# Gate and up projections as Strassen quads over both token halves, and a down projection that stays in PSUM

## The chip, the cores and the metric

The kernel runs on one core of one Trainium2 chip. The time is the device time of one execution in microseconds (us), and the number that counts is the median of several runs. All that is said of single instructions comes from one profiled execution of the kernel before. The engines are PE (TensorE, the matmuls), DVE (VectorE), ACT (ScalarE), POOL (GpSimd) and SP (SyncE, which issues the DMAs).

## The reference

Two transformer layers and a second block run over 1024 tokens of width 1024. Each layer has a mixer and a gated feed-forward part (FFN); the second block has an mLSTM branch and an S5 branch, whose recurrence needs tables made from its parameters.

```python
def swiglu(h, w_gate, w_up, w_down):
    return (jax.nn.silu(h @ w_gate) * (h @ w_up)) @ w_down      # 1024 -> 2816 -> 1024

for layer in range(2):
    h = rmsnorm(x, mix_pre_g[layer])
    m = even_mixer(h, ...) if layer == 0 else odd_mixer(h, ...)  # odd: (gelu(gate) * rg_lru(conv(xr))) @ w_out
    x = x + rmsnorm(m, mix_post_g[layer])
    h = rmsnorm(x, ffn_pre_g[layer])
    x = x + rmsnorm(swiglu(h, ...), ffn_post_g[layer])
# second block: h = x + rmsnorm((g1 * mlstm(...) + g2 * s5(...)) @ w_o)
# s5: a = exp(lam * dt), s_t = a * s_(t-1) + q B u_t, y = Re(C s) + D u
```

## The kernel before, in words

Features lie on the partitions, and the tokens are two halves of 512. Every fp32 operand is held as a high and a low part, so that the product of a 128x128 block of weights with a 128x512 block of activations is three matmuls (L151, L152, L153: high by high, high by low, low by high). A "unit" is 128 output features of one half: 24 matmuls for a depth of 1024.

Weights come by one DMA for each unit into a tile `raw` (two buffers), are rounded to the high part by ACT (L137), and DVE makes the low part (L139) into `wsp` (four buffers). Activations are split in the same way by `split` (L161 on ACT, then L165 on DVE or L163 on POOL or DVE).

`ffn` (L355) takes one half at a time. It makes the gate unit `pg` and the up unit `pu` of 4 or 6 hidden tiles, splits the hidden tiles (L161, L165), and then multiplies this group by its part of the down weights: 8 output units `pd`, each added to an fp32 tile `macc` in SBUF by DVE (L385). Four to six such groups make one half. The rmsnorm of the other half's next input runs beside the last group.

Work beside the matmuls comes from Python generators. `start(g, rate)` puts one in a list, each `tick` emits `rate` further steps of it, and `drain(g)` emits all that is left at once. The order of emission is the order of priority by which a scheduler fills the queue of each engine; a queue is then worked off in order. `early(n)` gives instructions an earlier priority (the loads and splits of weights).

The tables of the S5 branch come from the generator `s5_tables` (L952). It has a head of small DVE instructions, then a loop on DVE, ACT and PE over 16 groups (transposes and products `s5pt`, `s5pk` on PE, tiles `s5zr`, `s5zf`, `s5W`, `s5E`), and at last tables of rotations `s5R` on POOL alone (L1104 to L1117), two groups at a time. Before, it is started here:

```python
        self.layer0(lambda h, *m: self.finish(h, *m, "mix_post_g", 0), side)
        bg = self.start(self.s5_tables(), 1.5)
        self.ahead = 90
        self.drain(first[0])
        self.drain(ffn(0, 1, ("mix_pre_g", 1), (2, 4, 4, 4, 4, 4)))
        self.drain(bg)
```

The mixer of layer 1 follows. Of each head it makes two conv input units `pxr`, two gate units `pg` and the recurrence. `gelu2` (L448) is ACT, POOL (a `tensor_scalar`, L453), DVE, ACT, DVE in a row on a tile `gl`; the PSUM bank of `pg` is free only after its last step.

Of the kernel before, what the change touches and what calls it, by code (L numbers as in the profile page):

```python
# [21 lines left out]
NT = 8  # L22
T = 512
# [13 lines left out]

class Model:
    def __init__(self, ctx, tc, io, slots=24, nraw=2, nwsp=4, nt2=12):
# [3 lines left out]
        self.nslots, self.nraw, self.nwsp, self.nt2 = slots, nraw, nwsp, nt2  # L43
# [17 lines left out]
    def tick(self, n=1):  # L61
        """Emit the next steps of every background generator, each at its own rate."""
# [41 lines left out]
    def t2(self, name, shape=(128, T), dt=F32, tag="t2", bufs=None):  # L104
        return self._t(shape, dt, tag, bufs or self.nt2, name)
# [19 lines left out]
    def wtile(self, src, first=False):  # L125
        """src: [128, nk, n] in DRAM. Returns a tile [128, (hi, lo), 8, 128]."""
        nc = self.nc
        nk = src.shape[1]
        with self.early(self.ahead):
            raw = self.p.tile([128, 8, 128], F32, tag="raw", bufs=self.nraw, name="raw")[:, :nk]  # L130
            nc.sync.dma_start(raw, src)
        with self.early(self.ahead):
            sp = self.p.tile([128, 2, 8, 128], F32R, tag="wsp", bufs=self.nwsp, name="wsp")
            if first:
                nc.gpsimd.tensor_scalar(sp[:, 0, :nk], raw, 1.0, 0.0, ALU.mult, ALU.add)
            else:
                nc.scalar.activation(sp[:, 0, :nk], raw, AF.Copy)  # L137
        with self.early(self.ahead):
            nc.vector.tensor_tensor(sp[:, 1, :nk], raw, f(sp[:, 0, :nk]), ALU.subtract)  # L139
        return sp  # L140

# [3 lines left out]
    def mm3(self, ps, sp, xs, wk0=0, order=None, part=(0, None), bg=0):  # L145
        """ps (+)= the three products of every pair of tiles; part: which of them, in their order."""
        nc = self.nc
        order = order or range(len(xs))
        for i, k in list(enumerate(order))[slice(*part)]:
            h, l = sp[:, 0, wk0 + k], sp[:, 1, wk0 + k]  # L150
# [6 lines left out]
    def split(self, src, name, scale=1.0, dst=None, low=None):  # L157
        """hi/lo pair of src*scale (src fp32 in SBUF or PSUM)."""
# [10 lines left out]
    def sumsq_step(self, acc, src):  # L169
        nc = self.nc  # L170
        q = self.t2("sq", tag="sq", bufs=2)
# [1558 lines left out]
```

## Time and profile before

| | before |
|---|---|
| median of 3 timed runs | 3301.34 us (3300.61 to 3302.1) |
| span of the profiled execution, first to last instruction | 3297.8 us |
| PE busy | 3226.6 us, 98% |
| DVE busy | 2109.4 us, 64% |
| ACT busy | 1383.9 us, 42% |
| POOL busy | 380.3 us, 12% |
| mean granted clock of PE | 0.995 |

The span is that of one execution, without what lies ahead of its first and behind its last instruction; the median is 3.5 us longer, and this difference is taken as what lies around the span. A busy share is a mean over stages that have different limits, so the stage that a change touches is read by itself.

### The profile page before, as it was taken

Reading aid. Unit: us, or ns where it says so; the run is one execution under the profiler, and the core shown is the slowest. Engines: PE = TensorE matmul, PEld = TensorE weight load, DVE = VectorE, ACT = ScalarE, POOL = GpSimd, SP = SyncE. Lnnn points to the kernel's source line nnn. Section 1 sums busy time; section 2 is a strip of 40 time slices with the busy share of each in tenths; the row PEclk is TensorE's granted clock in tenths of the full one; section 3 lists DMA queues with packets and bytes.
Section 4 is the critical chain, followed back from the end, with each engine's and each line's share of the span. In section 5 each row is a group of like instructions: output and inputs, shape, how many; then the busy total and the mean of one; then the engine's idle time right before and its main releaser. Section 6 shows DMA issues by size and latency. Waiting matters only on the chain.

```text
span 3297.8 us, 41400 instructions
## 1 busy us (share of the span) xinstructions
PE 3226.6 (98%) x14848; PEld 2636.9 (80%) x14848; DVE 2109.4 (64%) x3911; ACT 1383.9 (42%) x2228; POOL 380.3 (12%) x720
## 2 busy tenths in 40 slices
PE   8999999999999999999999999999999999999998
PEld 5777788888788887878888888887888888788786
DVE  8668748667965479596544553348688888633633
ACT  4646544334522247575322332224455444323322
POOL 4011100000393002011000000000111110100000
PEclk9999999999999999999999999999999999999999
DMA  5444324434534344334433343237545444334533
GB/s 179 131 138 136 103 90 142 128 114 140 191 111 139 104 124 144 102 122 134 147 96 97 121 141 97 89 107 251 184 128 177 135 153 149 123 97 158 160 93 102
DMA packets 186429, 435.20 MB, mean 132 GB/s; under 512 B 23400, under 2 KB 48168, under 8 KB 186224
## 3 DMA queue, kind: packets, MB, share of 16 engines
q1 hardware_dynamic: 186224, 432.56, 41.8%
q8 instruction: 117, 1.92, 0.2%
q14 instruction: 88, 0.72, 0.1%
HBM read 364.19 MB, written 64.06 MB: 130 GB/s over the span
## 4 chain that ended last, share of the span: by engine, by line
PE 79%; DVE 11%; issue 4%; ACT 3%; DMA 2%; POOL 1%; SPq 0%; DVEq 0%; ACTq 0%; POOLq 0%
PE pg L153 6%; PE pg L152 6%; PE pg L151 6%; PE pu L151 5%; PE pu L153 5%; PE pu L152 5%; PE pd L152 4%; PE pd L153 4%; PE pd L151 4%; PE po L152 3%; PE po L151 3%; PE po L153 3%; DVE wsp L139 2%; PE pya L152 1%; PE pya L153 1%
## 5 line engine op out<-in xcount | busy, mean ns | idle before, releaser
L137 ACT ACTIVATE wsp<-raw 128x1024 fp32r<-128x1024 f32 (+3 forms) x614 | 566.1, 923 | 1161.6 <-issue 332.2
L139 DVE TENSOR_TENSOR wsp<-raw,wsp 128x1024 fp32r<-128x1024 f32 (+3 forms) x618 | 680.6, 1103 | 544.0 <-ACT wsp L137 539.7
L151 PE MATMUL pg<-xs,wsp 128*128 128x512 f32 x1088 | 425.3, 391 | 4.8 <-DVE xc L443 2.7
L152 PE MATMUL pg<-xs,wsp 128*128 128x512 f32 x1088 | 424.9, 391 | 1.1 <-POOL xs L163 1.1
L153 PE MATMUL pg<-xs,wsp 128*128 128x512 f32 x1088 | 424.6, 390 | 0.9 <-DVE wsp L139 0.9
L151 PE MATMUL pu<-xs,wsp 128*128 128x512 f32 x760 | 297.4, 391 | 0.0
L152 PE MATMUL pu<-xs,wsp 128*128 128x512 f32 x760 | 296.4, 390 | 0.0
L153 PE MATMUL pu<-xs,wsp 128*128 128x512 f32 x760 | 296.3, 390 | 0.0
L151 PE MATMUL pd<-hid,wsp 128*128 128x512 f32 x704 | 275.8, 392 | 0.5 <-DVE th L370 0.4
L152 PE MATMUL pd<-hid,wsp 128*128 128x512 f32 x704 | 275.3, 391 | 0.8 <-DVE hid L165 0.6
L153 PE MATMUL pd<-hid,wsp 128*128 128x512 f32 x704 | 274.3, 390 | 0.0
L151 PEld LDWEIGHTS pg<-xs,wsp 128*128 128x128 f32 x1088 | 204.3, 188 | 48.5 <-issue 3.4
L152 PEld LDWEIGHTS pg<-xs,wsp 128*128 128x128 f32 x1088 | 204.3, 188 | 45.1 <-POOL xs L163 2.7
L153 PEld LDWEIGHTS pg<-xs,wsp 128*128 128x128 f32 x1088 | 204.3, 188 | 43.3 <-DVE wsp L139 1.6
L163 POOL TENSOR_TENSOR xs<-xt,xs 128x512 fp32r<-128x512 f32 x36 | 54.2, 1504 | 1408.8 <-ACT xs L161 1393.0
L370 DVE TENSOR_TENSOR th<-th,pu 128x512 f32<-128x512 f32 x88 | 60.4, 687 | 179.0 <-PE pu L153 178.6
L153 PEld LDWEIGHTS pu<-xs,wsp 128*128 128x128 f32 x760 | 142.6, 188 | 29.7
L152 PEld LDWEIGHTS pu<-xs,wsp 128*128 128x128 f32 x760 | 142.7, 188 | 28.8
L151 PEld LDWEIGHTS pu<-xs,wsp 128*128 128x128 f32 x760 | 142.8, 188 | 28.7
L152 PEld LDWEIGHTS pd<-hid,wsp 128*128 128x128 f32 x704 | 132.2, 188 | 31.9 <-DVE hid L165 5.3
L151 PEld LDWEIGHTS pd<-hid,wsp 128*128 128x128 f32 x704 | 132.1, 188 | 28.3 <-ACT hid L161 0.8
L153 PEld LDWEIGHTS pd<-hid,wsp 128*128 128x128 f32 x704 | 132.2, 188 | 27.1
(637 smaller groups left out, 6620.0 us busy)
## 6 DMA issues: line engine op xcount, KB each, us to landing
raw<-in_w_in_dram SPq DMA_DIRECT2D x96, 512.0 KB
raw<-in_wg_dram SPq DMA_DIRECT2D x88, 512.0 KB
raw<-in_wu_dram SPq DMA_DIRECT2D x88, 512.0 KB
xt<-xres SPq DMA_DIRECT2D x120, 256.0 KB
raw<-in_wd_dram SPq DMA_DIRECT2D x96, 256.0 KB
raw<-in_wd_dram SPq DMA_DIRECT2D x48, 384.0 KB
raw<-in_ev_in_dram SPq DMA_DIRECT2D x32, 512.0 KB
xres<-xt SPq DMA_DIRECT2D x64, 256.0 KB
```

The source lines that it names most:

```text
L137: nc.scalar.activation(sp[:, 0, :nk], raw, AF.Copy)
L139: nc.vector.tensor_tensor(sp[:, 1, :nk], raw, f(sp[:, 0, :nk]), ALU.subtract)
L151: nc.tensor.matmul(ps, h, xs[k][:, 0], start=i == 0, stop=False)
L152: nc.tensor.matmul(ps, h, xs[k][:, 1], start=False, stop=False)
L153: nc.tensor.matmul(ps, l, xs[k][:, 0], start=False, stop=i == len(xs) - 1)
L163: (low or nc.vector).tensor_tensor(t[:, 1], src, f(t[:, 0]), ALU.subtract)
L370: nc.vector.tensor_tensor(th, th, pu, ALU.mult)
```

## The change

**Gate and up.** The units are now made in quads: two units by both token halves by both halves of the depth, by a form of Strassen's product with 7 instead of 8 products of half the depth (12 matmuls each). Operands are sums of weight blocks (`wquad`: four 128x512 sums on POOL for each quad) and sums of activations (`sum_steps`: DVE and POOL, with new splits). A quad makes 84 matmuls where there were 96. Both halves of x must be there for this, so six of the eleven pairs of hidden tiles (`ffn_first`) are begun with half 0 alone while half 1 is finished; one product of these is kept in DRAM (`m1d`), and the rest of such a quad is 5 products. There are 22 quads in each of the two layers.

**Down.** Hidden tiles go to DRAM (`hidd`), are loaded again (`hid_steps`, tile `hl`), and are split there. `ffn_down` adds all 22 of them in one PSUM bank, so the additions to `macc` go.

**Buffers.** `t4` has 27 slots instead of 24, `t2` 18 instead of 12, and takes in the tiles that had tags of their own (`xt`, `sq`, `hf`, `p`, `P`); `raw` has 3, `wsp` 8 of half the size, and weights are split in halves of 128x512.

**S5 tables.** The loop takes 2 groups of parameters at a time instead of 4, and the rotations 1 group instead of 2: twice as many instructions of half the size. The generator is started beside `ffn_down` alone, and what is left is emitted at once behind it.

```diff
+    def prod(self, ps, w, xs, start, bg):
...
+        for k in range(n):
+            h, l = w.h(k), w.l(k)
+
+            nc.tensor.matmul(ps, h, xs[k][:, 0], start=start and k == 0, stop=False, skip_group_check=not start)
+            nc.tensor.matmul(ps, h, xs[k][:, 1], start=False, stop=False, skip_group_check=not start)
+            nc.tensor.matmul(ps, l, xs[k][:, 0], start=False, stop=k == n - 1, skip_group_check=not start)
...
+    def quad(self, w, B, sink, bank, m1=None, bg=0.3):
+
+        nc = self.nc
+        Y, Z, X = bank("qy"), bank("qz"), bank("qx")
+        rest = m1 is not None
+        cp = lambda o, i: nc.scalar.activation(o, i, AF.Copy)
+        if not rest:
+            self.prod(Y, w["a11"], B["b11"], True, bg)
+            m1 = self.t2("qm1")
+            cp(m1, Y)
+        self.prod(Z, w["s1"], B["t1"], True, bg)
+        v5 = self.t2("qv5")
+        cp(v5, Z)
+        self.prod(Y, w["s2"], B["t2"], rest, bg)
...
+        self.prod(Z, w["s4"], B["b22"], False, bg)
+        sink(0, 1, Z, u2)
+        self.prod(Y, w["s3"], B["t3"], False, bg)
...
+        nc.gpsimd.tensor_tensor(v5, v5, u3, ALU.add)
+        sink(1, 1, v5, None)
...
+            self.prod(X, w["a12"], B["b21"], True, bg)
+            sink(0, 0, X, m1)
+            self.prod(Y, w["a22"], B["t4"], False, bg)
+            sink(1, 0, Y, None)
...
+    def hid_steps(self, h, out):
+        for j in range(FFT):
+            t = self.t2("hl")
+            self.nc.sync.dma_start(t, self.hidd[h][j])
+            out.append(self.split(t, "hid", 0.5))
+            yield
...
+    def ffn_down(self, l, h, hid, n0=0):
...
+                for k in range(n):
+                    h_, l_, x = sp.h(k), sp.l(k), hid[k0 + k]
+                    nc.tensor.matmul(ps, h_, x[:, 0], start=k0 + k == 0, stop=False)
+                    nc.tensor.matmul(ps, h_, x[:, 1], start=False, stop=False)
+                    nc.tensor.matmul(ps, l_, x[:, 0], start=False, stop=k0 + k == FFT - 1)
+                    self.tick(1 / 8)
+            nc.scalar.activation(mt, ps, AF.Copy)
+            ss = self.sumsq_step(ss, mt)
...
+    def ffn(self, l, B, keep, pre, hook, F, done=0, beside=()):
...
+        for j in range(done, F):
+            if j == done + 3:
+                self.finished()
+                nb = self.start(self.ffn_sums(*pre, B, keep), 1.0)
+            self.ffn_first(l, 2 * j, B, None)
+        self.drain(nb)
...
+        for j in range(F, n):
+            self.ffn_quad(l, 2 * j, B, False)
+        for j in range(F):
+            if j == F - 1:
+                nb = self.start(self.hid_steps(0, hid[0]), 3.0)
+            self.ffn_quad(l, 2 * j, B, True)
+        self.drain(nb)
+        self.ahead = 90
+        bg = self.start(beside, 2.0) if beside else None
+        m, ss = self.ffn_down(l, 0, hid[0])
+        hid[0].clear()
+        nb = self.start(self.hid_steps(1, hid[1]), 3.0)
+        self.drain(nb)
+        self.finish(0, m, ss, "ffn_post_g", l)
+        nb = self.start(chain(self.after(self.fin), hook()), 1.0)
+        m, ss = self.ffn_down(l, 1, hid[1])
+        self.drain(nb)
+        if bg:
+            self.drain(bg)
+        self.finish(1, m, ss, "ffn_post_g", l)
...
+        GT = 2
...
-        for g0 in range(0, 16, 2):
-            R = self.t4("s5R", [128, 2, 2, 256], F32)  # (gt, cos/sin, b)
+        for g0 in range(16):
+            R = self.t2("s5R", [128, 1, 2, 256])
...
-        bg = self.start(self.s5_tables(), 1.5)
-        self.ahead = 90
-        self.drain(first[0])
-        self.drain(ffn(0, 1, ("mix_pre_g", 1), (2, 4, 4, 4, 4, 4)))
-        self.drain(bg)
-        # layer 1 mixer
+        self.ffn(0, B[0], keep[0], ("ffn_pre_g", 0), hook("mix_pre_g", 1), 6, 1, self.s5_tables())
```

How the change moves instructions is seen in the queues at the border between layer 0's FFN and layer 1's mixer. On POOL of the kernel before, the last rotations stand ahead of four splits of the normed x (`xs`, two of them left out here), and then come the mixer's first two gelu steps (`gl`):

```order
L1115 TENSOR_TENSOR s5rt_10164<-s5R_10161,s5c_4840 128x256
L1116 TENSOR_TENSOR s5rt_10164<-s5R_10161,s5c_4840 128x256
L1117 TENSOR_TENSOR s5R_10161<-s5rt_10164 128x2x128
L163 TENSOR_TENSOR xs_10973<-xt_10970,xs_10973 128x512
...
L163 TENSOR_TENSOR xs_11131<-xt_11128,xs_11131 128x512
L453 TENSOR_SCALAR gl_11302<-gl_11302 128x512
L453 TENSOR_SCALAR gl_11345<-gl_11345 128x512
L163 TENSOR_TENSOR yo_11429<-gl_11302,yo_11429 128x512
```

On POOL of the changed kernel, the same two steps (now L710) stand among and behind the rotations of all 16 groups; first the place of `gl_12488`, then that of `gl_12531`, the last rotation ahead of it:

```order
L1371 TENSOR_TENSOR s5R_12238<-s5rt_12241 128x4
L1369 TENSOR_TENSOR s5rt_12294<-s5R_12291,s5c_8430 128x4
L1370 TENSOR_TENSOR s5rt_12294<-s5R_12291,s5c_8430 128x4
L710 TENSOR_SCALAR gl_12488<-gl_12488 128x512
L1371 TENSOR_TENSOR s5R_12079<-s5rt_12082 128x64
L1371 TENSOR_TENSOR s5R_12132<-s5rt_12135 128x32
...
L1373 TENSOR_TENSOR s5rt_12294<-s5R_12291,s5c_8430 128x128
L1374 TENSOR_TENSOR s5R_12291<-s5rt_12294 128x128
L710 TENSOR_SCALAR gl_12531<-gl_12531 128x512
L235 TENSOR_TENSOR yo_12615<-gl_12488,yo_12615 128x512
```

All 800 instructions on the `s5R` and `s5rt` tiles have moved behind the tables' loop: 676 of them stand ahead of `gl_12488` and the other 124 between it and `gl_12531`.

On PE of the kernel before, the last down products (`pd`) are followed by the mixer's first unit:

```order
L151 MATMUL pd_11153<-hid_10939,wsp_11121 128x512
L152 MATMUL pd_11153<-hid_10939,wsp_11121 128x512
L153 MATMUL pd_11153<-hid_10939,wsp_11121 128x512
L151 MATMUL pxr_11180<-xs_10973,wsp_11172 128x512
L152 MATMUL pxr_11180<-xs_10973,wsp_11172 128x512
```

On PE of the changed kernel, transposes and products of the tables' loop stand between the mixer's first units; these are the last of them, behind the first gate unit `pg_12444` and ahead of the second, `pg_12494`, with the statistics (`sst`, `rb`) of FFN half 1 between:

```order
L225 MATMUL pg_12444<-xs_10811,wsp_12433 128x512
L1342 MATMUL s5pk_11040<-s5zf_8433,s5zf_8432 128x128
L1343 MATMUL s5pk_11040<-s5zf_8433,s5zf_8432 128x128
L1340 MATMUL s5pt_11072<-ident_66,s5zf_8432 128x128 x2
...
L1342 MATMUL s5pk_11477<-s5zf_8433,s5zf_8432 128x128
L1343 MATMUL s5pk_11477<-s5zf_8433,s5zf_8432 128x128
L257 MATMUL sst_12470<-ones2_71,sq_10906 128x2 x4
L293 MATMUL rb_12519<-ident_66,nr_12476 128x128 x4
L223 MATMUL pg_12494<-xs_10394,wsp_12438 128x512
```

Ten of the sixteen groups of the loop have moved from the FFN to this place, and the mixer's matmuls behind them keep their order.

## Rows read from the trace of the kernel before

**Rows 1.** The page: the span, then busy time of each engine.

```profile
span 3297.8 us, 41400 instructions
PE 3226.6 (98%) x14848; PEld 2636.9 (80%) x14848; DVE 2109.4 (64%) x3911; ACT 1383.9 (42%) x2228; POOL 380.3 (12%) x720
```

**Rows 2.** Windows: from:to, length, busy PE, PEld, DVE, ACT, POOL, clock, DMA, GB/s.

```profile
440.00:1190.00 750.00, 744.42 (x3329) 611.40 (x3328) 485.37 (x1179) 270.68 (x468) 142.51 (x406) 1.00 0.41 126
1190.00:1520.00 330.00, 314.35 (x1382) 254.78 (x1381) 274.45 (x424) 219.70 (x315) 57.23 (x41) 0.99 0.41 132
1520.00:2265.00 745.00, 744.86 (x3308) 616.48 (x3307) 352.40 (x472) 234.55 (x318) 13.13 (x9) 1.00 0.39 121
```

**Rows 3.** Timeline of PE, first and last of 38 matmuls in a row: start, length.

```profile
2239.83 0.39 PE L153 MATMUL pd<-hid,wsp 128*128 128x512 f32 x1
...
2248.22 0.39 PE L151 MATMUL pd<-hid,wsp 128*128 128x512 f32 x1
```

**Rows 4.** Groups by shape: count, busy us, mean ns, idle ahead.

```profile
L137 ACT ACTIVATE wsp<-raw 128x512 fp32r<-128x512 f32 x138 | 86.8, 630 | 296.1 <-issue 84.5 <-PE pd L153 73.2 <-PE pya L153 51.2
L139 DVE TENSOR_TENSOR wsp<-raw,wsp 128x512 fp32r<-128x512 f32 x138 | 98.4, 714 | 57.5 <-ACT wsp L137 56.5
L165 DVE SCALAR_TENSOR_TENSOR hid<-th,hid 128x512 fp32r<-128x512 f32 x88 | 62.4, 709 | 2.0 <-ACT hid L161 1.4
L163 POOL TENSOR_TENSOR xs<-xt,xs 128x512 fp32r<-128x512 f32 x36 | 54.2, 1504 | 1408.8 <-ACT xs L161 1393.0 <-issue 8.4 <-PE pd L153 7.3
```

**Rows 5.** The chain of work that ended last: start, us, what.

```profile
1957.14 3.65 DMA xres<-xt
1960.86 2.58 DMA xt<-xres
```

**Rows 6.** The window in which POOL makes most of the rotations.

```profile
868.00:1010.00 142.00, 139.99 (x629) 115.15 (x628) 99.83 (x152) 50.10 (x84) 112.33 (x345) 1.00 0.52 164
```

**Rows 7.** Groups of DVE in 440 to 1010 us, small tiles of the tables.

```profile
L946 DVE TENSOR_TENSOR s5tp<-s5tp 128x64 f32<-128x64 f32 x32 | 7.1, 220 | 0.4
L1099 DVE TENSOR_TENSOR s5zr<-s5kf,s5zr 32x128 fp32r<-32x128 f32 x16 | 4.7, 292 | 0.9 <-ACT s5zr L1098 0.8
L947 DVE TENSOR_TENSOR s5c<-s5c 128x16 f32<-128x16 f32 x12 | 2.1, 173 | 0.3
```

**Rows 8.** Timeline of DVE: first instructions of two complex products in a row.

```profile
701.10 0.22 DVE L944 TENSOR_TENSOR s5tp<-s5c,s5W 128x64 f32<-128x64 f32 x1
...
702.15 0.22 DVE L944 TENSOR_TENSOR s5tp<-s5c,s5E 128x64 f32<-128x64 f32 x1
```

**Rows 9.** Groups of POOL in 868 to 1035 us, rotations by size.

```profile
L1113 POOL TENSOR_TENSOR s5rt<-s5R,s5c 128x2 f32<-128x2 f32 x8 | 1.5, 190 | 0.0
L1115 POOL TENSOR_TENSOR s5rt<-s5R,s5c 128x16 f32<-128x16 f32 x8 | 1.7, 212 | 0.2
L1113 POOL TENSOR_TENSOR s5rt<-s5R,s5c 128x64 f32<-128x64 f32 x8 | 2.3, 288 | 0.0
L1112 POOL TENSOR_TENSOR s5rt<-s5R,s5c 128x128 f32<-128x128 f32 x8 | 3.2, 397 | 0.2
```

**Rows 10.** Timeline of POOL: a pair of rotations interleaved, then one alone.

```profile
881.38 0.56 POOL L1112 TENSOR_TENSOR s5rt<-s5R,s5c 128x2 f32<-128x2 f32 x1 [6.20 <-DMA s5w<-s5wt]
...
885.04 0.19 POOL L1115 TENSOR_TENSOR s5rt<-s5R,s5c 128x4 f32<-128x4 f32 x1
885.20 1.18 POOL L1116 TENSOR_TENSOR s5rt<-s5R,s5c 128x4 f32<-128x4 f32 x1
...
906.51 1.06 POOL L1112 TENSOR_TENSOR s5rt<-s5R,s5c 128x256 f32<-128x256 f32 x1
...
916.08 0.52 POOL L1112 TENSOR_TENSOR s5rt<-s5R,s5c 128x2 f32<-128x2 f32 x1
...
931.19 0.61 POOL L1112 TENSOR_TENSOR s5rt<-s5R,s5c 128x256 f32<-128x256 f32 x1
```

**Rows 11.** A window at the end of the kernel, columns as in rows 2.

```profile
3270.00:3298.00 28.00, 13.34 (x67) 11.08 (x65) 11.31 (x25) 3.21 (x6) 6.04 (x4) 0.75 0.19 75
```

More of the change, by code (lines that the diff above doesn't have):

```diff
@@ new lines, in norm_keep @@
+    def norm_keep(self, h, gname, gi, B, keep):
+        nc = self.nc
+        pb = self.bcast(self.r[h])
+        B["b11"], B["b21"] = [], []
+        for k in range(NT):
+            t = self.t2("xt")
+            nc.sync.dma_start(t, self.x[h][k])
+            nc.vector.scalar_tensor_tensor(t, t, self.col(gname, gi * NT + k), pb, ALU.mult, ALU.mult)
+            nc.sync.dma_start(keep[k], t)
+            B["b11" if k < NT // 2 else "b21"].append(self.split(t, "xs", low=nc.vector if k % 2 else nc.gpsimd))
+            yield
@@ new lines, in ffn_quad, with whole, gate, up @@
+    def ffn_quad(self, l, j, B, rest):
+        nc, io = self.nc, self.io
+        g = {}
+        def whole(a, b):
+            if b is None:
+                return a
+            t = self.t2("qt")
+            nc.vector.tensor_tensor(t, a, b, ALU.add)
+            return t
+        def gate(i, h, a, b):
+            a = whole(a, b)
+            t = g[i, h] = self.t2("th")
+            nc.scalar.activation(t, a, AF.Tanh, scale=0.5)
+            nc.vector.scalar_tensor_tensor(t, t, 1.0, a, ALU.add, ALU.mult)
+        def up(i, h, a, b):
+            t = g[i, h]
+            nc.vector.tensor_tensor(t, whole(a, b), t, ALU.mult)
+            nc.sync.dma_start(self.hidd[h][j + i], t)
+        for i, (a, sink) in enumerate(((io["wg"], gate), (io["wu"], up))):
+            m1 = None
+            if rest:
+                m1 = self.t2("m1")
+                nc.sync.dma_start(m1, self.m1d[j + i])
+            self.quad(self.wquad(a[l, j], a[l, j + 1], rest), B, sink, self.pa if i else self.ps, m1)
@@ L395, in log1p_exp, with after @@
+    def after(self, g):
+        while any(e[0] is g for e in self.bg):
+            yield
     def log1p_exp(self, x, shape):
@@ L955, in s5_tables @@
         V, G = nc.vector, nc.gpsimd
-        big = self.t4("s5c", [128, 64, 16], F32)
+        big = [self.t2("s5c", [128, 32, 16]) for _ in range(2)]
         used = [0]
@@ L1119, in s5_tables @@
                     yield
-            for i in range(2):
-                nc.sync.dma_start(self.s5r[g0 + i], R[:, i])
+            nc.sync.dma_start(self.s5r[g0], R[:, 0])
             yield
@@ L1654, in run @@
                 self.finished()
-                xs[0] = []
-                nb = self.start(self.norm_steps(0, "ffn_pre_g", 1, xs[0]), 1.2)
+                nb = self.start(self.norm_keep(0, "ffn_pre_g", 1, B[1], keep[1]), 1.2)
             self.finish(h, *self.proj_out(io["od_out"], y[h]), "mix_post_g", 1, rate=0.5 if h == 0 else 1)
@@ L1659, in run @@
         self.ahead = 90
[L1660 to L1661 removed]
+        self.ffn(1, B[1], keep[1], ("ffn_pre_g", 1), hook("norm_pre_g_2", 0), 6)
         self.ahead = 90
```

288 lines of the change are left out of this document (194 added, 94 removed).

## The prediction

> **What bounds the kernel now.** The page comes first: PE is busy for 3226.6 of 3297.8 us [rows 1]. A mean hides stages, so the windows come next. In the FFN of layer 1 PE is busy for 744.86 of 745 us, in that of layer 0 for 744.42 of 750, at a granted clock of 1.00, while DVE is at 352 and 485 us, ACT at 235 and 271 and POOL at 13 and 143; the mixer between them has 16 us without PE in 330 [rows 2]. In the FFN, then, only PE's matmuls count as long as nothing else grows past them. The price of one is read from the starts in a row: 37 steps from 2239.83 to 2248.22 us, 0.2267 us each, though a row's own length says 0.39 [rows 3].
>
> What the FFN of layer 0 hides is as important as what it does: the S5 tables. POOL makes the rotations for 112 us of a 142 us window, in which PE is busy for 140 [rows 6]. Nobody waits for them there, and the mixer's gelu is still far off in POOL's queue.
>
> **The matmuls removed.** A quad has 84 where there were 96, and there are 22 quads in each layer: 2 x 22 x 12 = 528 fewer. At 0.2267 us that is 119.7 us, if PE stays the bound in the quads. For a product of 12 matmuls (2.72 us) ACT has to make one weight half, 0.63, and a bank copy of about that price; for a whole quad of 84 matmuls (19.0 us) DVE has six or seven weight halves at 0.714 and some adds, POOL five sums at 1.504 [rows 3, 4]. All stay below two thirds of PE's time. I take no stall here; if each bank copy came half a microsecond late in all 260 products of the quads, that would be 130 us, the bound on this side.
>
> **New transitions.** The quads want half 1 first, so half 0's units can't cover everything. For each layer: (a) finishing half 1, its statistics and the sums; of the 16 new POOL operations at 1.504 us (24 us) [rows 4] and the trips through DRAM at 2.6 to 3.7 us [rows 5] about two thirds lie beside the last three first pairs; 16 us are left by the order of the queues. (b) The last hidden tile goes out and comes back, one trip: 3 us. (c) Between the two down projections, 22 hidden tiles are loaded and split: 22 x 0.709 on DVE with eight weight halves at 0.714 is 21.3 us [rows 4], against 78 matmuls, 17.7 us; with the wait for the first one 7.5. (d) 2 us at the end. That makes 28.5 us a layer, 57 in all; bounds 25 (all DMA trips hidden) and 100 (all of (a) bare).
>
> **The tables that are left over.** Here most of the time is decided. The generator now gets its ticks from the down projections alone: 8 x 22 / 8 = 22 ticks for a half, 44 in all, 88 steps at rate 2. The order shows what that does not reach: ten of the sixteen groups of the loop and all 800 POOL instructions of the rotations. They are emitted behind the last down product and ahead of the mixer, and the queues keep that order.
>
> *A, the loop.* On PE the transposes of ten groups stand between `pxr` and the second gate unit; each waits for DVE. DVE has some 440 table instructions there. One group is 28 of a complex product (128x32), 4 subtractions, 6 copies, and the block of `s5zr`. The trace has no 128x32 form: 0.173 us at 16 elements and 0.220 at 64 bound it from both sides, and the largest are 0.292 [rows 7]. By durations a group is 9.5 us; but starts in a row are closer, six instructions in 1.05 us, 0.175 for 0.220 [rows 8], which gives about 7.9. So ten groups are 79 to 95 us, and 20 us of weight halves and norm steps lie between them. PE has some 76 matmuls to do meanwhile, 17 us. The stall is between 62 and 98; I take 75, near the lower end, since the products are mostly of the kind in rows 8.
>
> *B, the rotations ahead of the first gelu.* POOL can begin in earnest only when the loop has released its buffers, so B follows A. Of its 676 instructions some 640 are left by then. One group is 50: sizes 1, 2, 4 to 128, six each, two memsets. Clean rows are 0.190 (2), 0.212 (16), 0.288 (64), 0.397 (128) [rows 9]: about 11.5 us for a group by durations and 9.7 by starts, since a start follows the last by 0.04 to 0.05 less (885.04 to 885.20). Some rows are longer (1.18 instead of 0.19), and with these a pair took 25.1 us up to its last size, 82 instructions; one alone 15.1 for 42 [rows 10]. So 640 are 124 us clean, 175 to 195 as disturbed as before, 215 as one alone. I take 130, near the clean end, because DVE, beside which the long rows stand, has little to do while everything waits for this gelu. PE meanwhile has 72 to 80 matmuls (one gate unit, the recurrence, one `pxr`), then `pxr_12683` needs the bank of `pg_12444`, the unit of that gelu: 17 us. Stall 113, bounds 105 and 198.
>
> The Trainium skill (SBUF — State Buffer, "Who interferes with whom") says that a VectorE instruction with two SBUF inputs and a GpSimd instruction that reads SBUF exclude each other for the whole instruction. By that, B with VectorE idle goes at the clean price, 124 us, and the sum would be 6 us lower. The row at 885.20, where POOL's 0.19 became 1.18, agrees so far as one row can.
>
> *C, ahead of the second gelu.* The other 124 instructions, of the larger sizes, and the gelu step: 24 to 35 us; PE has 24 matmuls, 5.4 us. Stall 25.
>
> Everything else queued on POOL behind this (the `yo` splits, the splits of the next norm) comes later by the same time, but for PE it is the same wait. On DVE the finish of half 1 stands behind the loop; it is wanted only by half 1's mixer, far behind.
>
> **Clock.** A bare PE loses its clock: in the last 28 us, with PE busy for half of them, the granted clock is 0.75 [rows 11], while a full FFN has 1.00 [rows 2]. Three long pauses then cost some matmuls at half speed: I take 5 us, bounds 0 and 15.
>
> **Small things.** Weights are split in halves, 0.63 and 0.714 for each [rows 4]: some 0.2 us more on ACT and DVE for a unit outside of the FFN, beside PE. Fewer weight loads (64 of 512 KB) and more trips of activations about cancel. The additions to `macc` go from DVE, which was not the bound. I put all this at nothing; without cover (DVE is at 274 of 330 us in the mixer [rows 2]) it is up to 10 us.
>
> **Sum.** Span 3297.8 and 3.5 around it give 3301.3, the median. 3301.3 - 119.7 + 57 + 75 + 113 + 25 + 5 = 3456.6; I say **3455 us**, 4.7% slower.
>
> **Rivals.**
> - *The tables' rest does not hold PE.* Then 3301.3 - 119.7 + 57 = 3239 us, faster. It turns at one point: A, B and C together below 62.7 us. For it: the FFN before did hide all of this. Against it: in the queue of POOL the first gelu stands behind all of it, and 640 instructions in under 80 us would be 0.125 each, where the shortest clean row is 0.190 and the closest starts are 0.15. Only the loop on PE (A) could be mostly covered. Chance 7%; with a range of 3190 to 3290.
> - *The rotations go as disturbed as before.* The price of rows 10 for B, 175 to 215 us, gives 45 to 85 more, and 5 to 10 in C: 3505 to 3550. For it: DVE has its own backlog (the finish, weight halves) that it works off meanwhile. Against: this backlog is 20 to 30 us. Chance 15%.
> - *The quads or the transitions stall too.* A bank copy queued behind weight halves on ACT, or (a) laid bare: 40 to 100 more, 3500 to 3555. Against it: the sums of each engine. Chance 13%.
> - *Shorter A and B.* Chains overlap better than in rows 8, and B at 124 from an earlier start: A 50, B 95: 3410. Within the forecast.
>
> **How the numbers follow.** The forecast, with its own range of 3400 to 3500, has 63%; the first rival 7, the second 15, the third 13; 2% for no change, in which the rest about eats what the matmuls give. The 80% range reaches from 3390 to 3535: the lower end leaves out the first rival and no change (9%), the upper end the tails of the second and third (about 9%). What a measurement can tell from no change is about 0.2%, 6.6 us. Faster 0.08, same 0.01, slower 0.91.
>
> **What would show it.** In the profile after: 528 fewer PE matmuls at the same 0.227 us; quads with PE at 98% or more; pauses of PE near the end of layer 0's FFN of about 75, 113 and 25 us, the second put down to POOL or to the DVE step of `gl` behind it; POOL nearly all busy there for 150 us with rotations at about 0.2 us each; 25 to 30 us of PE idle at the borders of each FFN. The prediction is wrong if POOL reaches the first gelu within 60 us of the last down product, or if the window of the quads shows PE below 95%.

## The result, and the profile after

The changed kernel takes 3509.52 us (median of 4 runs, 3508.5 to 3510.84) where the kernel before, beside it, took 3300.98 (3300.46 to 3302.1). The ratio is 1.0629, with an interval of 1.0614 to 1.0644: 6.3% slower. The profiled execution has a span of 3506.7 us, and PE's mean granted clock is 0.948 (0.995 before).

The page of the changed kernel: the span, busy time and instructions of each engine, and of the 40 slices (tenths of busy time, 88 us each) those of PE, POOL and PE's clock. It answers to [rows 1].

```profile
span 3506.7 us, 42646 instructions
PE 3166.6 (90%) x14320; PEld 2569.4 (73%) x14320; DVE 2281.0 (65%) x4599; ACT 1516.2 (43%) x2780; POOL 772.5 (22%) x1362
...
PE   8999987999999712799979999999899999999998
...
POOL 4011103456200069311124364000011010100100
PEclk9999997999999855899989999999999999999999
```

PE has 528 instructions fewer, as many as the quads save, and yet is idle for 340 us, where it was 71 before. Most of the loss is in one place, the 15th and 16th slices, where PE falls to 1 and 2, its clock to 5, and POOL rises to 6 and 9. The windows (columns as in rows 2) show the quads of layer 0 first, then this place in steps of 50 us.

```profile
650.00:900.00 250.00, 250.00 (x1105) 206.89 (x1104) 172.09 (x197) 89.87 (x153) 131.54 (x84) 1.00 0.34 111
1200.00:1250.00 50.00, 13.57 (x54) 10.03 (x54) 43.01 (x268) 15.27 (x50) 2.04 (x14) 0.58 0.29 99
1250.00:1300.00 50.00, 6.07 (x24) 4.89 (x24) 17.92 (x78) 4.69 (x16) 40.83 (x232) 0.50 0.09 33
1300.00:1350.00 50.00, 0.00 (x0) 0.00 (x0) 0.00 (x0) 0.00 (x0) 50.00 (x278) 0.50 0.07 26
1350.00:1400.00 50.00, 15.14 (x51) 12.03 (x52) 9.05 (x15) 8.05 (x12) 49.84 (x215) 0.60 0.10 37
```

The quads run at full pace, 250.00 of 250 us. From 1200 to 1250 DVE works (the tables' loop) and everyone else waits; from 1300 to 1350 only POOL works, 278 rotations in 50 us. PE's own timeline (start, length, in brackets the idle time ahead and its releaser) shows the loop's step and then the long pause:

```profile
1217.58 0.66 PE L1340 MATMUL s5pt<-ident,s5zf 128*128 128x128 f32 x2 [8.61 <-DVE s5zf L1328]
1234.48 0.66 PE L1340 MATMUL s5pt<-ident,s5zf 128*128 128x128 f32 x2 [8.61 <-DVE s5zf L1328]
...
1264.62 1.09 PE L293 MATMUL rb<-ident,nr 128*128 128x128 f32 x4 [3.21 <-DVE nr L286]
1375.27 0.76 PE L223 MATMUL pg<-xs,wsp 128*128 128x512 f32 x1 [109.57 <-DVE l1h L702]
```

Two groups of the loop take 16.9 us (1217.58 to 1234.48), 8.45 each. The pause of 109.57 us is put down to `l1h`, the last step of the mixer's conv on DVE, which frees the PSUM bank of `pxr`. It is not the gelu. Who held the conv is told by the waits of ACT, DVE and POOL from 1185 to 1475 us (line waited for: total us, times, longest), and by ACT's timeline:

```profile
ACT xc L695 <- DMA s5r<-s5R: 94.4, 1, 94.4
DVE xc L698 <- ACT xc L695: 100.5, 2, 87.0
DVE gl L711 <- POOL gl L710: 37.1, 2, 28.9
POOL s5R L1361 <- DVE s5zr L1356: 67.4, 1, 67.4
```

```profile
1357.25 0.78 ACT L695 ACTIVATE xc<-pxr,pvt 128x512 f32<-128x512 f32 x1 [94.39 <-DMA s5r<-s5R]
1371.53 0.78 ACT L695 ACTIVATE xc<-pxr,pvt 128x512 f32<-128x512 f32 x1 [13.50 <-POOL s5R L1374]
```

The conv's first instruction writes a tile `xc` of the shared buffer `t2`. Its slot was that of a rotation table `s5R`, and came free only when that table was made and its store to DRAM had landed. The second `xc` waited in the same way for a slot that POOL freed. POOL in turn could not begin until 1242.87, when the loop released the slots for `s5R` (67.4 us). It came to the first gelu step later than this, ten us behind the end of PE's pause:

```profile
1384.86 0.63 POOL L710 TENSOR_SCALAR gl<-gl 128x512 f32<-128x512 f32 x1
```

Two further places differ. PE's waits over the whole changed kernel:

```profile
PE pg L223 <- DVE l1h L702: 125.4, 3, 109.6
PE pf L463 <- ACT m L544: 36.4, 2, 18.6
...
PE qz L463 <- ACT st L233: 20.2, 5, 4.8
...
PE mpo L223 <- ACT mu L1515: 8.9, 1, 8.9
```

The 36.4 us of `pf` are two pauses, one in each FFN, while half 1 is finished. ACT's timeline at the first one, and one row of DVE's:

```profile
522.95 0.63 ACT L244 ACTIVATE sq<-xt 128x512 f32<-128x512 f32 x1 [3.65 <-DVE xt L380]
526.65 0.63 ACT L244 ACTIVATE sq<-xt 128x512 f32<-128x512 f32 x1 [3.07 <-DVE xt L380]
531.06 0.63 ACT L244 ACTIVATE sq<-xt 128x512 f32<-128x512 f32 x1 [3.78 <-DVE xt L380]
531.60 1.06 ACT L544 ACTIVATE m<-pf 128x512 f32<-128x512 f32 x2
```

```profile
522.23 0.69 DVE L380 TENSOR_TENSOR xt<-xt,m 128x512 f32<-128x512 f32 x1 [2.20 <-DMA xt<-in_x_dram]
```

The load of a tile stands in SP's queue behind the store of the one before, which waits for DVE's addition, so that a step takes some 4 us; ACT waits for each in turn, and the copy `m` that would free PE's bank stands behind the last square in ACT's queue. PE stood from 514.46 to 532.23.

The sum of the differences, by the first PE instruction of each stage: up to the FFN of layer 0 -6 us, that FFN -12 (769 to 757), the mixer of layer 1 **+214** (332 to 546), the FFN of layer 1 -5 (725 to 720), the second block +18. That makes +209, the whole loss.

### The profile page after: what moved, and what is told of

It reads as the page before. It is cut to its first block, busy times and chain, and to the rows that moved or that the text cites. A ratio compares the mean times of both kernels' runs of the same rounds, so it can differ in the third digit from the quotient of the medians.

```text
span 3506.7 us, 42646 instructions
## 1 busy us (share of the span) xinstructions
PE 3166.6 (90%) x14320; PEld 2569.4 (73%) x14320; DVE 2281.0 (65%) x4599; ACT 1516.2 (43%) x2780; POOL 772.5 (22%) x1362
## 5 line engine op out<-in xcount | busy, mean ns | idle before, releaser
L175 DVE TENSOR_TENSOR wsp<-raw,wsp 128x512 fp32r<-128x512 f32 x890 | 645.1, 729 | 506.2 <-ACT wsp L173 502.2
L173 ACT ACTIVATE wsp<-raw 128x512 fp32r<-128x512 f32 x882 | 542.4, 617 | 894.1 <-PE pd L607 220.8
L223 PE MATMUL pg<-xs,wsp 128*128 128x512 f32 x384 | 153.5, 400 | 135.4 <-DVE l1h L702 125.4
L223 PEld LDWEIGHTS pg<-xs,wsp 128*128 128x128 f32 x384 | 74.1, 193 | 153.0 <-issue 110.6
L463 PE MATMUL qy<-st,wsp 128*128 128x512 f32 x432 | 170.0, 394 | 0.0
L465 PE MATMUL qy<-st,wsp 128*128 128x512 f32 x432 | 168.9, 391 | 0.0
L464 PE MATMUL qy<-st,wsp 128*128 128x512 f32 x432 | 168.8, 391 | 0.0
L224 PE MATMUL pg<-xs,wsp 128*128 128x512 f32 x384 | 152.5, 397 | 0.0
L225 PE MATMUL pg<-xs,wsp 128*128 128x512 f32 x384 | 152.3, 397 | 0.0
L495 POOL TENSOR_TENSOR qv<-qv,qu 128x512 f32<-128x512 f32 x44 | 68.8, 1564 | 298.8 <-ACT qu L473 150.4
L246 DVE TENSOR_TENSOR sq<-sq 128x512 f32<-128x512 f32 x140 | 98.8, 707 | 52.9 <-ACT sq L244 52.5
L173 ACT ACTIVATE wsp<-wss 128x512 fp32r<-128x512 f32 x88 | 55.6, 632 | 148.8 <-PE qy L465 64.0
L197 POOL TENSOR_TENSOR wss<-raw 128x512 f32<-128x512 f32 x44 | 60.7, 1380 | 224.3 <-DMA raw<-in_wg_dram 176.5
L463 PE MATMUL pf<-xs,wsp 128*128 128x512 f32 x192 | 76.5, 402 | 37.0 <-ACT m L544 36.4
```

The lines of the kernel that those rows point to most:

```text
L173: nc.scalar.activation(sp[:, 0], raw, AF.Copy)
L175: nc.vector.tensor_tensor(sp[:, 1], raw, f(sp[:, 0]), ALU.subtract)
L223: nc.tensor.matmul(ps, h, xs[k][:, 0], start=i == 0, stop=False)
L224: nc.tensor.matmul(ps, h, xs[k][:, 1], start=False, stop=False)
L225: nc.tensor.matmul(ps, l, xs[k][:, 0], start=False, stop=i == len(xs) - 1)
L246: nc.vector.tensor_tensor(q, q, acc, ALU.add)
```

## The experiments

The theory after the profile was that the rotations hold the mixer because of where they stand, and that PE's small pauses come from `finish`. The lengths of stages, in us, from the first PE instruction of one kind to that of the next (first pairs, quads, down products, mixer; a dash where a kernel isn't cut so):

| kernel | time | ratio, interval | first pairs 0 | quads 0 | down 0 | mixer | first pairs 1 | quads 1 | down 1 | block 2 |
|---|---|---|---|---|---|---|---|---|---|---|
| before | 3301 | | - | - | - | 332 | - | - | - | 1026 |
| changed | 3509.5 | 1.0629 | 145 | 377 | 257 | 546 | 90 | 374 | 255 | 1045 |
| s5_early | 3441.7 | 1.0418, 1.0402 to 1.0434 | 146 | 452 | 305 | 360 | 90 | 374 | 255 | 1043 |
| gelu_on_dve | 3514.9 | 1.0635, 1.0619 to 1.0651 | 145 | 377 | 259 | 555 | 90 | 374 | 253 | 1045 |
| residual_prefetch | 3453.2 | 1.0449, 1.0433 to 1.0464 | 132 | 376 | 258 | 541 | 76 | 374 | 255 | 1031 |
| own_rotation_slots | 3503.5 | 1.0611, 1.0594 to 1.0627 | 144 | 377 | 390 | 410 | 90 | 374 | 256 | 1044 |
| own_slots_gelu_dve | 3512.6 | 1.063, 1.0615 to 1.0644 | 144 | 377 | 391 | 413 | 92 | 375 | 256 | 1052 |
| tables_in_two_parts | 3419.5 | 1.0349, 1.0335 to 1.0363 | 146 | 378 | 256 | 343 | 90 | 374 | 342 | 1070 |
| tables_in_three_parts | 3399.6 | 1.0291, 1.0276 to 1.0306 | 145 | 388 | 329 | 348 | 90 | 374 | 265 | 1042 |
| three_parts_prefetch | 3335.5 | 1.0094, 1.008 to 1.0107 | 133 | 388 | 327 | 333 | 75 | 374 | 262 | 1032 |
| three_parts_prefetch_cover | 3326.9 | 1.0068, 1.0054 to 1.0082 | 158 | 360 | 327 | 330 | 91 | 353 | 262 | 1033 |
| rotations_spread | 3266.8 | 0.9884, 0.9867 to 0.99 | 157 | 360 | 264 | 332 | 91 | 354 | 264 | 1033 |

Block 2 is taken up to the last PE instructions. The first pairs of layer 0 begin with one that is made some 22 us ahead of the FFN's stage. The two kernels made from the kernel before have their numbers in the text.

**The same tables, early.** The generator is started ahead of the quads.

```diff
+        bg = self.start(beside, 3.0) if beside else None
         for j in range(F, n):
...
-        bg = self.start(beside, 2.0) if beside else None
         m, ss = self.ffn_down(l, 0, hid[0])
```

> The changed kernel, with the S5 tables' generator started ahead of the quads at rate 3 instead of beside the down projections at rate 2, so that next to nothing of it is left behind the last down product. If what was left over held PE for the 214 us by which the stretch from the mixer's first unit to the next FFN has grown, this comes to 3300 us (3285 to 3325) and that stretch to about 335 us. Rival: the tables crowd the quads instead (DVE there 257 us of 378 and some 100 more, POOL 179 and some 50 more): PE busy in the quads falls below 93%, 3330 to 3400. Second rival, the left-over tables are not the cause: above 3450.

Measured: 3441.7 us. The mixer gave back 186 us, and the quads and the down products of layer 0 took 123 of these again (377 to 452, 257 to 305). The place is decisive, but the theory's 3300 was too simple: the tables crowd what they stand beside. In the quads these are the head and the loop, with DVE busy for 119 of 150 us from 550 to 700; no rotation starts before 1052 us, in the down products. The crowding is larger than the rival's upper price.

**The named lock alone.** The gelu's step goes from POOL to DVE in the mixer.

```diff
-        nc.gpsimd.tensor_scalar(t, t, 0.044715, 1.0, ALU.mult, ALU.add)
+        (nc.vector if name == "gl" else nc.gpsimd).tensor_scalar(t, t, 0.044715, 1.0, ALU.mult, ALU.add)
```

> The changed kernel, with the one POOL step of the mixer's gelu moved to DVE; the tables stay where they are. If the order of POOL's queue is what PE waits for in the 110 us pause and the 32 us behind it, these go and the loop's pauses stay: 3370 us (3355 to 3395), with the rotations running on POOL beside the mixer. Rival: another POOL step (the splits of x or of the mixer's output) is wanted soon after and takes the wait over: 3430 to 3500.

Measured: 3514.9 us, no gain. PE's largest wait in this kernel:

```profile
PE pg L223 <- DVE l1h L702: 141.1, 3, 110.1
```

The pause is unchanged (110.1), so POOL's queue ahead of the gelu is not what held PE here.

**The place alone, in the kernel before.** No quads and no new buffers; the tables only start 22 steps of the FFN's generator later, so that the 400 (longer) instructions of the rotations are left when the mixer begins.

```diff
-        bg = self.start(self.s5_tables(), 1.5)
...
-        self.drain(ffn(0, 1, ("mix_pre_g", 1), (2, 4, 4, 4, 4, 4)))
+        second = ffn(0, 1, ("mix_pre_g", 1), (2, 4, 4, 4, 4, 4))
+        for _ in range(22):
+            next(second)
+        bg = self.start(self.s5_tables(), 1.5)
+        self.drain(second)
```

> The kernel before, with the start of the S5 tables alone moved: 22 steps into the second half's FFN, so that ten to twelve groups of the loop and all rotations stand behind the last down product, in their old sizes (400 POOL instructions instead of 800). If the place alone costs, some 11 groups of the loop at 8.5 to 9.5 us less 17 us under cover, and 350 POOL instructions at about 0.36 us less 17, make 3301 + 165 = 3466 us (3430 to 3500). Rival: the halved and doubled instructions are the cost, and the place is harmless: below 3360.

Measured: 3435.3 us, 1.0399 (1.0382 to 1.0417). From the first `pxr` to the second block's first unit it takes 1196 us, where the kernel before takes 1057. The late start alone costs 131 us, without anything else of the change. In this kernel the tables `s5R` have slots in another buffer (`t4`), and the lock of PE's longest pause is the one that the prediction named: the gelu step behind the rotations in POOL's queue, with `ra` behind it in ACT's.

```profile
1317.47 0.69 DVE L454 TENSOR_TENSOR gl<-gl,pg 128x512 f32<-128x512 f32 x1 [45.70 <-POOL gl L453]
1318.19 0.63 ACT L455 ACTIVATE gl<-gl 128x512 f32<-128x512 f32 x1 [47.19 <-DVE gl L454]
1320.88 0.80 PE L151 MATMUL pi<-xcs,wsp 128*128 128x512 f32 x1 [42.44 <-ACT ra L490]
```

**The residual tiles loaded ahead.** `finish` loads three tiles of x ahead instead of one at a time.

```diff
+            pre = []
+            for k in range(3):
+                pre.append(self.t2("xt"))
+                nc.sync.dma_start(pre[k], self.x[h][k])
...
-                t = self.t2("xt")
-                nc.sync.dma_start(t, self.x[h][k])
+            t = pre[k]
+            if not last and k + 3 < NT:
+                pre.append(self.t2("xt"))
+                nc.sync.dma_start(pre[k + 3], self.x[h][k + 3])
```

> The changed kernel, in which the residual add of each finish loads three tiles of x ahead instead of one behind the store of the tile before. If the pause of 18 us in each layer's first pairs and the 9 us in the second block come from this chain of DMA trips (4.1 us a tile, with copies of PSUM banks queued behind its squares on ACT), the pauses shrink by most of that: 3455 to 3480 us. Rival: the sums of the quads' operands pace this stretch, or the traffic on the DMA queues does: 3500 us and more.

Measured: 3453.2 us, 56 less. The pauses of `pf` fall from 36.4 to 8.5 us in all, and the 8.9 of `mpo` are gone:

```profile
PE pf L467 <- ACT m L548: 8.5, 3, 5.2
```

By stages it is 13 and 14 us in the first pairs and 14 in the second block. But 7 us of it lie ahead of the FFN of layer 0 and 5 in the mixer, where the kernel before has the same `finish`: not all of it is a cost of the change.

**Slots of their own for the rotations.** Four of `t2`'s 18 slots are set apart for `s5R` and `s5rt`, first with the gelu left on POOL, then with both edits.

```diff
-    def __init__(self, ctx, tc, io, slots=27, nt2=18):
+    def __init__(self, ctx, tc, io, slots=27, nt2=14):
...
-            R = self.t2("s5R", [128, 1, 2, 256])
+            R = self._t([128, 1, 2, 256], F32, "s5r", 4, "s5R")
...
-            tp = self.t2("s5rt", [128, 2, 1, 128])
+            tp = self._t([128, 2, 1, 128], F32, "s5r", 4, "s5rt")
```

> The changed kernel, with four slots of their own for the two tiles of a rotation, taken from the shared t2 slots (14 are left of 18); the gelu step stays on POOL. The run with that step on DVE kept its 110 us pause to the hundredth, with ACT's first tap of the mixer's convolution waiting for the store of a rotation: the slot of a t2 tile, not POOL's order. If there are two locks in a row, the slot and then POOL's order, this run changes the name of the wait but hardly the time: 3490 to 3520 us, and the long pause stands ahead of the unit that needs the bank of the first gate unit. If the slot was the only lock: 3380 to 3410.

> Both at once: the rotations in slots of their own, and the gelu's POOL step on DVE. With slot and queue order as the two locks, the 110 us pause and the 32 us behind it go, the loop's pauses stay, and the rotations run on POOL beside the mixer: 3370 us (3350 to 3400). Rival: a third lock (the splits on POOL, or the 14 slots that are left are too few): above 3440.

Measured: 3503.5 and 3512.6 us. The mixer fell from 546 to 410, but the down products of layer 0 rose from 257 to 390. The edit did more than free the conv: POOL no longer had to wait for the loop's slots, and made all 800 rotations by 1172 us, ahead of the loop's end and of the mixer (first `pxr` at 1316 and 1318). So these runs do not test the two locks in the mixer; they move the rotations, and another wait holds PE where they now stand. In the second of the two kernels, the waits from 926 to 1317 us, SP's queue and ACT's timeline:

```profile
SPq L1377 <- POOL s5R L1374: 64.8, 6, 14.9
...
ACT wsp L173 <- DMA raw<-in_wd_dram: 125.5, 9, 24.7
```

```profile
1093.61 12.22 SPq L1377 DMA_DIRECT2D s5r<-s5R x2
1105.95 0.35 SPq L162 DMA_DIRECT2D raw<-in_wd_dram x1
```

```profile
1109.67 1.15 ACT L173 ACTIVATE wsp<-raw 128x512 fp32r<-128x512 f32 x2 [23.23 <-DMA raw<-in_wd_dram]
```

A store of a rotation table waits in SP's queue until POOL has made it; the load of the next down weights stands behind it, and ACT is 23.23 us late with them. By the four rows of such stores, the first of which is shown, SP stood 187 us for POOL. That 14 shared slots are fewer than 18 was not tried by itself. The expectation of 3370 for both edits failed. The first run lies in its range (3490 to 3520), but not for the reason given: its long pause is not where it was expected.

**The tables in two parts.** The head and six groups stand beside the down products of layer 0 (rate 2), the rest and all rotations beside those of layer 1 (rate 4).

```diff
-        bg = self.start(beside, 2.0) if beside else None
+        bg = self.start(part_of(beside), RATES[l])
...
+            if g0 == SPLIT:
+                yield True
```

> The changed kernel with the tables made in two parts: the head and six groups of the loop beside layer 0's down projections as now, the other ten groups and all rotations beside layer 1's (rate 4), where DVE is busy for 125 us of 256 and POOL for 6; nothing is left ahead of the mixer. The mixer's stretch falls from 546 to about 340 us; the down projections of layer 1 take what moves there (85 us on DVE, 150 on POOL) at a cost of 0 to 20: 3310 us (3290 to 3335). Rival: the tables crowd whatever stage they lie beside, as they crowded the quads and down projections of layer 0 (122 us there): above 3380.

Measured: 3419.5 us. The mixer is back at 343, and what it gave is lost in part where the rotations now stand: the down products of layer 1 take 342 us instead of 255. Windows of this stretch:

```profile
2100.00:2200.00 100.00, 88.11 (x379) 70.61 (x378) 56.22 (x141) 38.29 (x77) 77.24 (x272) 0.93 0.46 157
2200.00:2330.00 130.00, 82.94 (x313) 65.34 (x313) 36.74 (x66) 25.60 (x49) 115.23 (x450) 0.82 0.34 114
```

POOL is busy for 115 of 130 us, DVE for 37 and ACT for 26: nobody else is near a limit, and PE still stands for a third of it.

**The finer weight splits, in the kernel before.** Each rounding and each difference is made in two halves.

```diff
-                nc.scalar.activation(sp[:, 0, :nk], raw, AF.Copy)
...
+        for a in range(0, nk, 4):
+            b = min(a + 4, nk)
...
+                    nc.scalar.activation(sp[:, 0, a:b], raw[:, a:b], AF.Copy)
```

> The kernel before, with each weight split of 128x1024 (and 128x768) made as two instructions of at most 128x512 on ACT and DVE, as the changed kernel has them. If these finer splits are why mixer and second block lost a few us outside of any long pause, 3307 to 3318 us. Rival: they lie beside PE and cost nothing: 3298 to 3304.

Measured: 3309.85 us, 1.0017 (1.0009 to 1.0026), some 5.6 us by the ratio and 4.5 by the medians: a cost, but a small one.

**The tables in three parts, then with the prefetch, then with more cover.** The head stands beside the quads of layer 0; the rotations and half of the loop beside its down products, the other half beside those of layer 1. Cover means nine and eight pairs begun with half 0 alone instead of six, and `finish` behind five of them instead of three.

```diff
+        bg = [self.start(self.s5_head(), 0.9)] if l == 0 else []
...
+        if l == 0:
+            bg = [self.start(self.s5_rot(), 2.2), self.start(self.s5_loop(0, 8), 1.4)]
+        else:
+            bg = [self.start(self.s5_loop(8, 16), 1.4)]
...
-            if j == done + 3:
+            if j == done + 5:
```

> The changed kernel with the tables cut into parts that each go slowly beside a long stage: the head beside layer 0's quads (0.9 steps a tick), the rotations (2.2) and the first half of the loop (1.4) beside layer 0's two down projections, the second half of the loop (1.4) beside those of layer 1. Theory: 800 rotations hurt only by the rate at which they are emitted, some 190 us of work on POOL in about 257 us of down projections here, and no loop of DVE and PE is left ahead of the mixer. Then the mixer of layer 1 comes back to about 340 us (it was 546), the down projections grow by at most 30 us, and the time is 3300 to 3340. Rival, by the run with the tables in two parts: that rotations in 260 us of a stage crowd out the weights and hidden tiles there wherever it is; then the down projections of layer 0 grow by 60 to 100 us and the time is 3380 to 3420. Pure placing, with nothing crowded, would give 3509 less 204, that is 3305.

> As tables_in_three_parts, and finish loads its residual tiles three ahead. Theory: the two causes are independent, so the gain of the prefetch alone (56 us) adds in full: 3245 to 3285, faster than the kernel before by 0.5 to 1.7%. Rival: the loads and stores of the rotations stand in the same queue of DMAs as the residual tiles, so that the gain shrinks to 20 to 30 us and the time is 3275 to 3310, that of the kernel before.

> As three_parts_prefetch, and more half-0 work ahead of the place where half 1 is needed: finish of half 1 and the sums begin behind five first pairs instead of three, and nine (layer 0) or eight (layer 1) pairs are begun with half 0 alone instead of six. If what is left of the transitions is a want of cover (the waits of the quads' operands on DVE and of the first units on the bank copy), it is 10 to 25 us faster than three_parts_prefetch. If it is the order of ACT's queue, it is the same within 5 us, since more cover moves the place and not the order.

Measured: 3399.6, 3335.5 and 3326.9 us. The first agrees with the rival (down products of layer 0 at 329, +72). The prefetch adds in full, 64 us where it gave 56 alone, so the rotations did not eat its gain; the total missed its range because the first part did. More cover gives 8.6 us, a little under the range, and a new pause is longer than that: PE waited 13.3 us once for `qu` on DVE, in the quads beside the head. The windows and waits of the last of the three say what the 70 us are (waits of 1040 to 1215 us):

```profile
920.00:1040.00 120.00, 115.37 (x510) 92.55 (x509) 70.33 (x249) 44.16 (x95) 101.36 (x346) 1.00 0.40 136
1040.00:1250.00 210.00, 152.91 (x632) 123.47 (x631) 114.43 (x331) 72.94 (x150) 141.20 (x460) 0.84 0.45 150
```

```profile
SPq L1400 <- POOL s5R L1397: 32.6, 3, 13.6
SPq L1400 <- POOL s5rt L1392: 28.2, 2, 14.8
SPq L1400 <- POOL s5R L1394: 17.2, 1, 17.2
SPq L1400 <- POOL s5R L1385: 15.3, 2, 10.1
...
ACT sq L244 <- POOL s5R L1385: 16.5, 1, 16.5
```

With POOL busy for 101 of 120 us, PE still ran at 115: a busy POOL by itself costs little. The pauses come where SP stands in stores (L1400) that wait for POOL, 93 us in this stretch by the four rows, with down weights, hidden tiles and residual tiles behind them, and where ACT waits for a slot that a rotation holds.

**The rotations spread out, their stores out of SP's queue.**

```diff
-            bg = [self.start(self.s5_rot(), 2.2), self.start(self.s5_loop(0, 8), 1.4)]
+            bg = [self.start(self.s5_rot(0, 8), 1.2), self.start(self.s5_loop(0, 8), 1.4)]
...
-            bg = [self.start(self.s5_loop(8, 16), 1.4)]
+            bg = [self.start(self.s5_rot(8, 16), 1.2), self.start(self.s5_loop(8, 16), 1.4)]
...
-            nc.sync.dma_start(self.s5r[g0], R[:, 0])
+            nc.gpsimd.dma_start(self.s5r[g0], R[:, 0])
```

> As three_parts_prefetch_cover, with two more edits to the rotations: eight of the sixteen groups go beside the down projections of layer 0 and eight beside those of layer 1 (1.2 steps a tick in each), and the store of a finished group is issued from POOL's queue and no longer from SP's, where in three_parts_prefetch_cover loads of down weights and of residual tiles stood behind stores that waited for POOL by 10 to 17 us each. Theory: with the stores out of SP's queue nobody waits for POOL's lag; the down projections of layer 0 come back from 327 to 260 to 275 us, those of layer 1 stay at 262 to 275, and the time is 3260 to 3285, faster than the kernel before. Rival: the slots of the shared buffer, which a group holds as long as POOL takes, are the lock that is left (ACT waited 16.5 us for one); then layer 0's down projections keep 290 or more, layer 1's grow by 20 to 30, and the time is 3310 to 3330, as without the edits. The run does not part the one edit from the other, save by the rows of the waits: a wait for an s5R slot on ACT or DVE speaks for the rival.

Measured: 3266.8 us, 0.9884 (0.9867 to 0.99): 1.2% faster than the kernel before, and 243 us faster than the change as it was made. Its two windows of down products:

```profile
920.00:1170.00 250.00, 240.84 (x1070) 195.56 (x1069) 173.45 (x563) 113.72 (x230) 138.62 (x416) 0.99 0.56 182
...
1960.00:2220.00 260.00, 249.98 (x1111) 202.54 (x1110) 179.02 (x568) 118.04 (x240) 140.48 (x416) 0.99 0.59 191
```

All 800 instructions are still made, now in two stretches in which POOL is busy for 139 and 140 us, most of it with them, beside a PE that is busy for 96%. Of waits for a rotation's slot ACT has one line left, 3.7 us in all. How much of it is the halved rate and how much the other queue isn't separated.

## Why the prediction was right, and where not

The time, 3509.5 us, lies in the range (3390 to 3535) and on the forecast side. It lies 55 us above the point and 10 above the forecast's own range of 3400 to 3500, within the ranges of the second and the third rival; the number alone can't tell them apart. By the steps:

- **Matmuls removed, -119.7.** Right: 528 fewer, and the quads at 250.00 of 250 us. The rival of late bank copies in the quads is out.
- **Transitions, 57.** The term was too small. The two FFNs are 12 and 5 us shorter where their matmuls alone would make them 49 and 60 shorter: of the 264 that layer 0 saves, 48 fall ahead of this stage, where more first units stood before. So the borders, with the slow matmuls there, cost some 37 and 55, about 92, and the stretch ahead of layer 0's FFN another 5. That is the third rival in part: (a) laid bare, at 35 to 40 us. PE's idle time in the two FFNs is 35.8 and 38.7 us, where it was 5.5 and 0.1. The part that failed is (a): "about two thirds lie beside the last three first pairs; 16 us are left". In layer 1 PE waits 18.6 us for `m` ahead of the quads, and 8.3 for the sums' operands in two pauses within the first of them, against 16 for all of (a). I had counted POOL's operations and single trips; the row of trips that follow on each other, eight tiles at 4 us with ACT's copy queued behind them, was the price. (b) and (c) came out smaller: PE's waits for `hid` on ACT are 5.9 us in all for both layers.
- **The rest of the tables, 213 (A 75, B 113, C 25).** The sum was right, but by luck: errors cancelled. The mixer grew by 214. Its pauses are 47 us in A, because part of the loop's first groups was already through when PE came to them; 109.6 in B; 32 in C (9.6, 9.3 and 12.9), of which only the 9.3 is put down to the gelu. These make 189, slower matmuls another 12, and the rest, some 13, is by exclusion the loop's own work on PE.
- **The price of the rotations** was right. From 1300 to 1350 us, with DVE at 0.00, 278 of them took 50.00 us, 0.18 each. Of POOL's groups in 1235 to 1470 us, two sizes that answer to [rows 9]:

```profile
L1373 POOL TENSOR_TENSOR s5rt<-s5R,s5c 128x128 f32<-128x128 f32 x16 | 6.4, 398 | 0.0
...
L1373 POOL TENSOR_TENSOR s5rt<-s5R,s5c 128x64 f32<-128x64 f32 x16 | 4.7, 292 | 0.0
```

  So the second rival (rotations as disturbed as in [rows 10]) is out: counted one by one in POOL's trace, none of 763 rotations between 1262 and 1418 us is longer than 0.8 us, and 24 of 345 are in the window of [rows 6]. Each of these 24 stands beside a DVE instruction with two inputs, most often a weight half (`wsp<-raw,wsp`). The Trainium skill (SBUF — State Buffer, "Who interferes with whom") lets only VectorE hold a GpSimd read; that the long rows go where VectorE is idle agrees with it.
- **The mechanism of B** was wrong. The step that failed is "`pxr_12683` needs the bank of `pg_12444`, the unit of that gelu". PE waited sooner: the second gate unit, `pg_12494`, needs the bank of the first `pxr`, the convs that free it wanted two slots of `t2`, and rotations held these, the first until its store had landed. gelu_on_dve shows that the gelu wasn't the lock of this pause; that the slot was is read from ACT's wait of 94.39 us, and no run frees the slot and leaves the rotations where they are. The slots came free at 1357 and 1371 us and the gelu's place at 1385, all as POOL worked its rotations off, which is why the size was nearly right (109.6 for 113) with the wrong lock. A repair by the predicted lock gained nothing. In the kernel before with late tables the predicted lock is the true one, as its rows show; what the prediction passed over is that the change moves `s5R` from `t4` into `t2`, the buffer of the conv's tiles. That this makes the difference between the two is argued, not tested by itself.
- **Clock, 5 (bounds 0 to 15).** Too small. Matmuls that start 0.36 to 0.6 us after the one before instead of 0.2267 make some 45 us in excess over the changed kernel (14 of it in the mixer), and 6 in the kernel before: 39 more. In the mixer, where the three long pauses are, it is 12 more, within the bounds; what the term left out is the many short pauses elsewhere. It overlaps with the terms above, in which it is counted.
- **Small things, 0.** Wrong by more than the 10 us of the bound: +18 in the second block. Of this the prefetch gives back 14 (8.9 of it the pause of `mpo`), and finer splits cost the kernel before some 5 over its whole length.
- **The first rival** (the tables' rest doesn't hold PE, 3239) did not come true, but rotations_spread shows that its time is nearly within reach: 3266.8 once the rest is spread out and the residual tiles come early.

By the measured terms: 3301.3 - 6 - 12 + 214 - 5 + 18 is 3510.

## What to carry to other kernels

When a stage that hid background work is made shorter, or loses its ticks, price that work at the place where it ends up; the kernel before, with its tables started late, loses 131 us without any other edit. A queue position names one lock; before you repair it, list everything that the late producer holds, which here were buffer slots and the stores in a queue that also carries loads, because with one of them free another may still hold. A load, an add and a store for each tile in turn cost the sum of the trips, and all that is queued on an engine behind the last of them pays it too.

## What was not expected of the hardware

- Short pauses of PE are dearer than their length. Behind the pause of 109.57 us, six matmuls start 0.42 to 0.57 us apart and one 0.39 before the step is 0.23 again; behind the next, of 9.59 us, the slow ones are fourteen. The timeline of PE there:

```profile
1375.84 0.63 PE L224 MATMUL pg<-xs,wsp 128*128 128x512 f32 x1
1376.26 0.63 PE L225 MATMUL pg<-xs,wsp 128*128 128x512 f32 x1
...
1378.59 0.39 PE L225 MATMUL pg<-xs,wsp 128*128 128x512 f32 x1
1378.82 0.39 PE L223 MATMUL pg<-xs,wsp 128*128 128x512 f32 x1
...
1396.05 0.80 PE L223 MATMUL pi<-xcs,wsp 128*128 128x512 f32 x1 [9.59 <-ACT ra L747]
...
1402.18 0.41 PE L225 MATMUL pxr<-xs,wsp 128*128 128x512 f32 x1
1402.43 0.40 PE L223 MATMUL pxr<-xs,wsp 128*128 128x512 f32 x1
```

  The granted clock of the window 1300 to 1350 is 0.50, that is the lower of the two levels (1.2 of 2.4 GHz), and PE did nothing in it; in the quads it is 1.00.
- A DMA that waits in SP's queue costs what stands behind it, not its own issue. Issuing the store in three_parts_prefetch_cover is 0.33 us, and SP stood up to 17.2 us for one. The Trainium skill (DMA: Bandwidth & Descriptors, "Issuing engines are not separate DMA queues") says that another issuing engine only saves the time of issue, usually small. That counts the issue alone; here the wait ahead of it was the cost. The run in which the stores went to POOL's queue was 60 us faster, but the rate of the rotations was halved in it too, so that the share of the queue stays open.
